# Two blocks of a transformer on one core: first products by token tile, and the rms norms as late factors

## Chip, cores and metric

The kernel runs on one core of a Trainium2 chip. The metric is the device time of one execution in microseconds (us); the median of the runs is given. The core's engines, each with a queue of its own that it works off in order, are TensorE (PE; its weight loads are PEld), VectorE (DVE), ScalarE (ACT), GpSimd (POOL) and SyncE (SP), which here issues the weight loads.

## What is computed

256 tokens of width 2048 and a context of 256 more pass through a first block of two layers, and the 256 tokens then through a second block. All is float32.

```python
# first block, layer l (layer 0 on x and ctx, layer 1 on x alone beside k and v of ctx)
h    = x * (1 + scale_l) + shift_l                 # scale, shift, gate from silu(c) @ w_mod[l]
parts = h @ w_in[l]                                # conv, q, k, v, gates, pool
out  = concat(conv, attention, pool) @ w_out[l]
x    = layernorm(ALPHA * x + gate_l * out) * ln_g[l] + ln_b[l]
# second block
hn = rms_norm(x, norm_mix_g)                       # x * rsqrt(mean(x*x) + 1e-6) * g
q_a, k_a, v_a, q_b, k_b, v_b, f, g_a, g_b = split(hn @ w_in_2)
merged = sigmoid(g_a) * (moba(q_a, k_a, v_a) @ w_proj_a) + sigmoid(g_b) * (fox(q_b, k_b, v_b, f) @ w_proj_b)
x  = x + merged @ w_out_2
hm = rms_norm(x, norm_mlp_g)
x  = x + square(relu(hm @ w_up)) @ w_down
return rms_norm(x, norm_final_g)
```

## The kernel before

Every weight passes once through the core. `fetch` (L171 to L187) loads a chunk of 128x1024 floats (two K tiles of 512 columns, or four of 256) and splits it: ScalarE casts it to a rounded half `hi` (L185), VectorE subtracts to get the residue `lo` (L186). Raw chunks, hi and lo have three buffers each. A product is three matmuls, hi·hi, hi·lo and lo·hi (`mm3`, L246 to L249). Activations lie transposed (channels on partitions) in `Act` tiles, again as hi and lo (`split`, L337).

Two routines do the products. `lin_b` (L251) holds blocks of 128 weight columns, and its result has channels on partitions and tokens along the row; with 256 tokens hi and lo of the activation go in one matmul, and VectorE sums the two halves afterwards (L306, L315). `lin_a` (L279) holds tiles of 128 tokens, and its result has tokens on partitions. Both go chunk by chunk, all blocks or tiles for one chunk, in five accumulators. With `hold=3` the last three chunks of a `lin_a` are done tile by tile, so that the first tile is ready before the last one.

The end of a layer is `mix_out` (L797): five column blocks, the last with hold 3; each tile's rows z get gate, residual and statistics (L818 to L820), and after the last block `ln_coef` (L826) makes mean and 1/std, with a power on GpSimd (L123). What follows must turn the rows into a transposed activation:

- Layer 0 to layer 1: `next_layer` (L902 to L925) scales the rows of all four tiles (L906 ScalarE, L908 VectorE), transposes (L913), applies gain and shift of the layer norm and of the modulation (L915, L916), splits (L339, L340); two steps run before layer 1's first products, six behind their chunks. GpSimd makes x1 = the x rows with gain and shift (L923, L924) and stores it.
- Layer 1 to the second block: `norm_rows` (L932) applies the layer norm to the rows with gain and shift (L945, L946; the last quarter of tile 1 by ScalarE and GpSimd), sums squares (L850) and makes the factor 1/rms. `norm_T` (L985) multiplies the rows by it (L992, L994), transposes (L1000) and splits (L1002, L1003). The first three residues of the group behind are GpSimd's.
- Before w_up: the same `norm_T`, once all of x is summed and squared (L1168, L850).

The order of the instructions on an engine is mainly the program's; a scheduler in the build moves some of them past others. Work between chunks is queued: `later` and `bg_step` run one step of a generator behind each chunk, `deferred` runs a function some chunk ends later.

## Time and profile before

| | |
|---|---|
| median of 3 runs | 2932.58 us (2932.4 to 2933.4) |
| profiled execution, its own time | 2930.09 us |
| span, first to last instruction | 2928.3 us |
| TensorE busy | 2871.4 us, 98% of the span |
| VectorE busy | 1946.9 us, 66% |
| ScalarE busy | 1179.6 us, 40% |
| GpSimd busy | 249.3 us, 9% |
| mean granted TensorE clock | 0.993 |

The span is 2.5 us below the median of the runs, so the two are not mixed. An engine that is busy 66% of the span may still be the one that is waited for in a short stretch: there one reads the waits and the order, not the share.

### The profile page before, as it was taken

The numbers are of one execution on the slowest core, as the hardware profiler recorded it, in microseconds if no ns is written. First come the engines' busy times: TensorE is split into PE (matmuls) and PEld (weight loads), VectorE is DVE, ScalarE is ACT, GpSimd is POOL, SyncE is SP. The second block draws the span as 40 slices with busy tenths as digits, with TensorE's granted clock in tenths as the row PEclk, the third lists the DMA queues.
The fourth block names the chain that finished last, engine by engine and source line by source line (L and its number), as shares of the span: only waits on it lengthen the run. The fifth ranks groups of instructions, "written<-read, shape, count | busy, mean of one in ns | idle before, by whom it ended". The sixth has DMA issues, their size and how long they took to land.

```text
span 2928.3 us, 38793 instructions
## 1 busy us (share of the span) xinstructions
PE 2871.4 (98%) x14898; PEld 2371.6 (81%) x14898; DVE 1946.9 (66%) x2890; ACT 1179.6 (40%) x1688; POOL 249.3 (9%) x287
## 2 busy tenths in 40 slices
PE   8999999999999999999969999999999999999998
PEld 5677777777879788888868888888888888888887
DVE  3779987887885658477675555766656556455564
ACT  3123432432322435244434454544445434344443
POOL 0000001001100410012110000001101101010011
PEclk9999999999999999999989999999999999999999
DMA  8764445455754445456744545455555555656554
GB/s 307 268 205 143 134 159 173 158 162 180 243 196 133 133 137 194 155 164 200 238 140 166 187 157 184 156 188 180 196 191 173 194 187 186 200 185 192 191 189 166
DMA packets 156433, 533.84 MB, mean 182 GB/s; under 512 B 17860, under 2 KB 21196, under 8 KB 156248
## 3 DMA queue, kind: packets, MB, share of 16 engines
q1 hardware_dynamic: 148656, 510.79, 52.8%
q0 software_dynamic: 5632, 18.36, 2.1%
q8 instruction: 116, 1.90, 0.3%
q10 hardware_dynamic: 1960, 2.22, 0.3%
q14 instruction: 69, 0.57, 0.1%
HBM read 527.07 MB, written 4.23 MB: 181 GB/s over the span
## 4 chain that ended last, share of the span: by engine, by line
PE 72%; issue 5%; DVE 3%; DMA 1%; ACT 1%; POOL 1%; POOLq 0%; ACTq 0%; DVEq 0%
PE acc L267 23%; PE acc L247 11%; PE acc L269 11%; PE acc L249 11%; PE acc L248 11%; PE aux L658 1%; PE aux L690 1%; DVE lo L186 1%; DVE ma L406 1%; PE aux L680 0%; POOL small L123 0%; PE aux L1077 0%; ACT hi L185 0%; DMA raw<-in_w_in_dram 0%; DVE small L660 0%
## 5 line engine op out<-in xcount | busy, mean ns | idle before, releaser
L186 DVE TENSOR_TENSOR lo<-raw,hi 128x1024 fp32r<-128x1024 f32 x766 | 937.2, 1227 | 679.2 <-ACT hi L185 676.9
L185 ACT CAST hi<-raw 128x1024 fp32r<-128x1024 f32 x769 | 805.5, 1050 | 1352.5 <-PE acc L249 457.9
L267 PE MATMUL acc<-act,hi 128*128 128x512 f32 x2960 | 1050.0, 399 | 0.7 <-DVE qs L306 0.7
L269 PE MATMUL acc<-act,lo 128*128 128x256 f32 x2960 | 829.3, 281 | 0.0
L267 PEld LDWEIGHTS acc<-act,hi 128*128 128x128 f32 x2960 | 555.2, 188 | 139.7 <-issue 5.1
L247 PE MATMUL acc<-hi,act 128*128 128x512 f32 (+1 forms) x1568 | 582.7, 372 | 1.5 <-ACT act L339 1.3
L249 PE MATMUL acc<-hi,act 128*128 128x512 f32 (+1 forms) x1568 | 578.3, 369 | 0.5 <-DVE act L340 0.5
L248 PE MATMUL acc<-lo,act 128*128 128x512 f32 (+1 forms) x1568 | 578.1, 369 | 0.2 <-DVE lo L186 0.2
L269 PEld LDWEIGHTS acc<-act,lo 128*128 128x128 f32 x2960 | 558.0, 189 | 1.8 <-DVE lo L186 0.2
L406 DVE SCALAR_TENSOR_TENSOR ma<-mod,cc,ma 128x512 f32<-128x512 f32 x480 | 339.1, 744 | 28.1 <-DMA mod<-in_w_mod_dram 26.7
L247 PE MATMUL acc<-act,hi 128*128 128x512 f32 x896 | 357.3, 399 | 0.0
L249 PE MATMUL acc<-act,lo 128*128 128x512 f32 x896 | 350.3, 391 | 0.0
L248 PE MATMUL acc<-act,hi 128*128 128x512 f32 x896 | 350.0, 391 | 0.0
L247 PEld LDWEIGHTS acc<-hi,act 128*128 128x128 f32 x1568 | 296.5, 189 | 54.9 <-issue 4.0
L249 PEld LDWEIGHTS acc<-hi,act 128*128 128x128 f32 x1568 | 296.2, 189 | 50.2 <-DVE act L340 1.1
L248 PEld LDWEIGHTS acc<-lo,act 128*128 128x128 f32 x1568 | 296.7, 189 | 49.4 <-DVE lo L186 1.2
L247 PEld LDWEIGHTS acc<-act,hi 128*128 128x128 f32 x896 | 168.2, 188 | 52.7 <-ACT hi L185 8.8
L249 PEld LDWEIGHTS acc<-act,lo 128*128 128x128 f32 x896 | 168.2, 188 | 39.1 <-issue 3.7
L248 PEld LDWEIGHTS acc<-act,hi 128*128 128x128 f32 x896 | 168.5, 188 | 35.7 <-issue 3.0
L315 DVE TENSOR_REDUCE tmp<-acc 128x256 f32<-128x512 f32 x169 | 112.8, 683 | 52.4 <-PE acc L269 52.4
L1184 POOL TENSOR_TENSOR tmp<-tmp 128x256 f32<-128x256 f32 x64 | 69.8, 1090 | 565.7 <-ACT tmp L1183 538.5
L340 DVE TENSOR_TENSOR act<-tmp,act 128x256 fp32r<-128x256 f32 (+1 forms) x96 | 58.4, 615 | 45.8 <-ACT act L339 45.7
(209 smaller groups left out, 1648.8 us busy)
## 6 DMA issues: line engine op xcount, KB each, us to landing
raw<-in_w_in_dram SPq DMA_DIRECT2D x384, 512.0 KB, 3.5
mod<-in_w_mod_dram SPq DMA_DIRECT2D x158, 512.0 KB, 4.2
raw<-in_w_up_dram SPq DMA_DIRECT2D x128, 512.0 KB, 4.3
raw<-in_w_down_dram SPq DMA_DIRECT2D x128, 512.0 KB, 4.3
raw<-in_w_out_dram SPq DMA_DIRECT2D x96, 512.0 KB, 4.3
mod<-in_w_mod_dram SPq DMA_DIRECT2D x68, 256.0 KB, 5.2
raw<-in_w_proj_a_dram SPq DMA_DIRECT2D x16, 512.0 KB, 3.5
raw<-in_w_proj_b_dram SPq DMA_DIRECT2D x16, 512.0 KB, 4.0
```

The lines of the kernel that those rows point to most:

```text
L185: S.copy(hi, raw)
L186: (fn or V).tensor_sub(lo, raw, hi)
L247: mm(ps, lh, rh, start=start, stop=False)
L248: mm(ps, lh, rl, start=False, stop=False)
L249: mm(ps, ll, rh, start=False, stop=stop)
L267: mm(p[:w, :].rearrange("p (a t) -> p a t", a=2), hi[:, kk, c:c + w], act.both(k0 + kk, tok), start=start, stop=False)
L269: mm(p[:w, :ntok], lo[:, kk, c:c + w], ah[:, tok], start=False, stop=stop)
L315: V.reduce_sum(t, ps[0], axis=AX.X)
L340: V.tensor_sub(lo, src, h)
L406: V.scalar_tensor_tensor(st[s], raw[:, kk, :], cc2[:, k, s:s + 1], st[s], op0=ALU.mult, op1=ALU.add)
L658: mm(p[:, :nk], a[r, q0:q0 + P], b[r, 0:nk], start=n == 0, stop=n == 2)
L1184: G.tensor_mul(t, t, t)
```

## The change

`lin_a` gets a `lead`: its first three chunks, too, can be done tile by tile, with a `hook` called behind each chunk of a tile. Where a new activation is needed, the rows of the early tiles are scaled and turned by such hooks, between products of the late tiles: behind layer 0, the context's tiles 0 and 1 between tile 3's last products; behind layer 1, tile 0 between tile 1's. `turn_T` turns two K tiles at a time. An `Act` takes its tiles one by one.

In the second block the norm's 1/rms no longer scales the rows. Gain and shift of layer 1's norm and the gain of the rms norm are applied to the transposed values (for the shift and gain, columns `lng1` and `lnb1` are added to the small parameters). x2 itself and its squares are made later (`norm_mix`). `row_factors` makes 1/rms as a row over the tokens, in all partitions, by a product of a matrix of ones with a diagonal; a product group's result is multiplied by it (tokens along the row) or scaled by the column (tokens on partitions). In w_up the relu becomes max and multiplication on VectorE. GpSimd makes no residues any more.

```diff
@@ lin_a, its callers' arguments left out
-    def lin_a(act, tiles, consume, korder=K16, mid=None, hold=1):
+    def lin_a(act, tiles, consume, korder=K16, mid=None, hold=1, lead=0, hook=None):
-        for ks in [[k] for k in korder[:cut]] + [korder[cut:]]:
+        for ks in [korder[:lead]][:lead] + [[k] for k in korder[lead:cut]] + [korder[cut:]]:
...
+                    if hook and len(ks) > 1:
+                        hook(i, ks.index(k0))
@@ first transition
+    def scale_rows(i, nt, z=z0):
+        t, (m, r, nb) = z[i, nt], z[i]
+        if i % 2:
+            S.activation(t, t, AF.Identity, scale=r, bias=nb)
+        else:
+            V.tensor_scalar(t, t, r, nb, op0=ALU.mult, op1=ALU.add)
+    def turn_T(act, z, tiles, kt, c1, c0, tok):
+        n = len(tiles)
+        ps, f = aux(), tmp(2 * n * P)
+        for k in range(2):
+            for j, i in enumerate(tiles):
+                o = (n * k + j) * P
+                nc.tensor.transpose(ps[:, o:o + P], z[i, kt // 4][:, (kt % 4 + k) * P:(kt % 4 + k + 1) * P], ident)
+        for k in range(2):
+            o = slice(k * n * P, (k + 1) * n * P)
+            g, b = c1[:, kt + k:kt + k + 1], c0[:, kt + k:kt + k + 1]
+            if k:
+                S.activation(f[:, o], ps[:, o], AF.Identity, scale=g, bias=b)
+            else:
+                V.tensor_scalar(f[:, o], ps[:, o], g, b, op0=ALU.mult, op1=ALU.add)
+        split(act.two(kt, tok), f.rearrange("p (k t) -> p k t", k=2))
...
+    def done0(i, z, cf):
+        z0.update(z)
+        z0[i] = cf
...
+        if i < 2:
+            for nt in range(2):
+                scale_rows(i, nt)
+        else:
+            scale_rows(i, 0)
...
+    def hook0(i, k):
+        if i == 3:
+            turn(2 * k, 0)
...
+    def lead0(i, k):
+        n = 3 * i + k
+        if n == 1:
+            for j in (2, 3):
+                scale_rows(j, 1)
+        elif n in (3, 4, 5):
+            turn(2 * (n - 3), 1)
+        elif n in (6, 7):
+            turn(6, n - 6)
+            for j in (2 * n - 12, 2 * n - 11):
+                scale_rows(j, 2)
+        elif n in (8, 9):
+            turn(8, n - 8)
...
+        turn(10, 0)
+        turn(10, 1)
+        for j in range(4):
+            scale_rows(j, 3)
+        yield
+        for kt in (12, 14):
+            turn(kt, 0)
+            turn(kt, 1)
+            yield
...
-            for i, (m, r, nb) in coef.items():
-                if i % 2:
-                    S.activation(z[i, nt], z[i, nt], AF.Identity, scale=r, bias=nb)
-                else:
-                    V.tensor_scalar(z[i, nt], z[i, nt], r, nb, op0=ALU.mult, op1=ALU.add)
-            for b in range(4):
-                kt = 4 * nt + b
-                ps = aux()
-                for i in range(4):
-                    nc.tensor.transpose(ps[:, i * P:(i + 1) * P], z[i, nt][:, b * P:(b + 1) * P], ident)
-                f = tmp()
-                S.activation(f[:, CTX], ps[:, CTX], AF.Identity, scale=fs[:, kt, 0:1], bias=fb[:, kt, 0:1])
-                V.tensor_scalar(f[:, X], ps[:, X], fs[:, kt, 1:2], fb[:, kt, 1:2], op0=ALU.mult, op1=ALU.add)
-                split(hT[kt], f)
-                if b % 2:
-                    yield
@@ second transition, its removed lines first
-    def norm_rows(i, z, coef):
-        ss = sums5()
-        m, r, nb = coef
-        for nt in POOLED[i]:
-            t = z[i, nt]
-            S.activation(t, t, AF.Identity, scale=r, bias=nb)
-            G.tensor_mul(t, t, lng1[nt])
-            G.tensor_add(t, t, lnb1[nt])
-        for nt in range(4):
-            t = z[i, nt]
-            if nt not in POOLED[i]:
-                V.scalar_tensor_tensor(t, t, m, lng1[nt], op0=ALU.subtract, op1=ALU.mult)
-                V.scalar_tensor_tensor(t, t, r, lnb1[nt], op0=ALU.mult, op1=ALU.add)
-                square_sum(t, ss, nt)
-        for nt in POOLED[i]:
-            square_sum(z[i, nt], ss, nt)
-        rs[i] = rms(ss)
...
+    def turn1(kt, *tiles):
+        turn_T(hn, z1, tiles, kt, gb1[:, :KT], gb1[:, KT:], slice(tiles[0] * P, (tiles[-1] + 1) * P))
+    def done1(i, z, cf):
+        z1.update(z)
+        z1[i] = cf
+        for nt in range(2):
+            scale_rows(i, nt, z1)
+    def hook1(i, k):
+        if i == 1 and k < 2:
+            turn1(2 * k, 0)
...
+    x2 = mix_out(1, Y, lambda i, nt: x1[i * P:(i + 1) * P, nt * 512:(nt + 1) * 512], done1, hook1)
+    turn1(4, 0)
...
+    def row_factors(n, ss, wait):
+        dg = []
+        for i in range(2):
+            rs[n, i] = rms(ss[i])
+            dg.append(tmp(P))
+            V.tensor_scalar(dg[i], ident, rs[n, i], None, op0=ALU.mult)
+        one = tmp(P)
+        G.memset(one, 1.0)
+        def spread():
+            p = aux()
+            for i in range(2):
+                mm(p[:, i * P:(i + 1) * P], one, dg[i], start=True, stop=True)
+            S.copy(rsr[n], p[:, :T])
+        deferred.append([wait, spread])
+    def lead1(i, k):
+        n = 3 * i + k
+        if n < 3:
+            turn1(2 * n, 1)
+        elif n == 3:
+            turn1(6, 0, 1)
+            for j in range(2):
+                scale_rows(j, 2, z1)
+        elif n == 5:
+            turn1(8, 0, 1)
+    def norm_mix():
+        ss = [sums5(), sums5()]
+        for j in range(2):
+            scale_rows(j, 3, z1)
+        for kt in (10, 12, 14):
+            turn1(kt, 0, 1)
+            yield
+        for nt in range(4):
+            for i in range(2):
+                t = x2[i, nt]
+                V.tensor_mul(t, t, lng1[nt])
+                V.tensor_add(t, t, lnb1[nt])
+                square_sum(t, ss[i], nt)
+            yield
+        row_factors(0, ss, 4)
+        for t, i in early:
+            S.activation(t, t, AF.Copy, scale=rs[0, i])
@@ the factors
     def norm_T(act, xs, rs, gain):
...
-                t = t32()
-                if i:
-                    S.activation(t, xs[i, nt], AF.Copy, scale=rs[i])
-                else:
-                    V.tensor_scalar(t, xs[i, nt], rs[i], None, op0=ALU.mult)
-                n.append(t)
...
-                S.activation(t, val(ps), AF.Copy, scale=HD_SCALE)
+                V.scalar_tensor_tensor(t, val(ps), HD_SCALE, rsr[0], op0=ALU.mult, op1=ALU.mult)
...
-            S.activation(t, val(ps), AF.Sigmoid)
+            V.tensor_mul(t, val(ps), rsr[0])
+            S.activation(t, t, AF.Sigmoid)
...
+        if (c0 + n) % 512 == 0:
+            later(norm_T(hm, x2, c0 // 512, "nlg"))
+    row_factors(1, ss, 6)
...
-                S.activation(t, val(ps), AF.Relu)
+                V.scalar_tensor_tensor(t, val(ps), 0.0, rsr[1], op0=ALU.max, op1=ALU.mult)
```

How the instructions stand, at the three places where waits are worked out below. First VectorE at the end of layer 0, from the coefficients of tile 2 on (L818 is L829 of the changed kernel, L186 is L185, L340 is L351). Before:

```order
L908 TENSOR_SCALAR p_6628<-p_6628,small 128x512 [waits DVE_49]
L908 TENSOR_SCALAR p_6960<-p_6960,small 128x512
L186 TENSOR_TENSOR lo<-raw,hi 128x1024 [waits DMAHW4_49,Activation_49]
L186 TENSOR_TENSOR lo<-raw,hi 128x1024 [waits DMAHW5_49,Activation_49]
L818 TENSOR_TENSOR tmp<-acc,row 128x256 [waits PE_49]
L186 TENSOR_TENSOR lo<-raw,hi 128x1024 [waits DMAHW6_49,Activation_49]
L819 SCALAR_TENSOR_TENSOR p_7556<-p_7556,tmp 128x256 [waits DVE_49]
L908 TENSOR_SCALAR p_7276<-p_7276,small 128x512
L820 BN_STATS bn<-p_7556 128x6 [waits DVE_49]
L908 TENSOR_SCALAR p_7554<-p_7554,small 128x512
```

After:

```order
L955 TENSOR_SCALAR tmp<-aux,fs,fb 128x256 [waits PE_49]
L939 TENSOR_SCALAR p_6631<-p_6631,small 128x512 [waits DVE_49]
L185 TENSOR_TENSOR lo<-raw,hi 128x1024 [waits DMAHW4_49,Activation_49]
L351 TENSOR_TENSOR act<-tmp,act 128x2x256 [waits DVE_49,Activation_49]
L955 TENSOR_SCALAR tmp<-aux,fs,fb 128x256 [waits PE_49]
L185 TENSOR_TENSOR lo<-raw,hi 128x1024 [waits DMAHW5_49,Activation_49]
L955 TENSOR_SCALAR tmp<-aux,fs,fb 128x256 [waits PE_49]
L829 TENSOR_TENSOR tmp<-acc,row 128x256
L185 TENSOR_TENSOR lo<-raw,hi 128x1024 [waits DMAHW6_49,Activation_49]
L351 TENSOR_TENSOR act<-tmp,act 128x2x256 [waits DVE_49,Activation_49] x2
L830 SCALAR_TENSOR_TENSOR p_7559<-p_7559,tmp 128x256 [waits DVE_49]
```

The scaled transposed pairs (L955) and their residues (L351) now stand among the residues of the next weights (L185), and tile 3's last column block (L829, L830) behind them.

Second, TensorE around the end of layer 1 (`acc_12959` and `acc_12962` are tile 1's last column block, `ident` marks a transpose, `hi_13177` the first weights behind). Before:

```order
L249 MATMUL acc_12959<-hi_12992,act_12307 128x256
L1000 MATMUL aux_13147<-ident_105,p32_13143 128x128 [waits DVE_49]
L1000 MATMUL aux_13152<-ident_105,p32_13143 128x128
L1000 MATMUL aux_13157<-ident_105,p32_13143 128x128
L1000 MATMUL aux_13147<-ident_105,p32_13145 128x128 [waits Activation_49]
L1000 MATMUL aux_13152<-ident_105,p32_13145 128x128
L1000 MATMUL aux_13157<-ident_105,p32_13145 128x128
L247 MATMUL acc_13173<-hi_13177,act_13141 128x512 [waits Activation_49]
```

After, still within tile 1's second of three held chunks:

```order
L246 MATMUL acc_12962<-hi_12965,act_12326 128x256
L948 MATMUL aux_13061<-ident_105,p32_12347 128x128 [waits DVE_49]
L948 MATMUL aux_13061<-ident_105,p32_12347 128x128
L247 MATMUL acc_12962<-lo_12966,act_12326 128x256
L248 MATMUL acc_12962<-hi_12965,act_12326 128x256
L948 MATMUL aux_13082<-ident_105,p32_12347 128x128 x2
L246 MATMUL acc_12962<-hi_12995,act_12326 128x256
```

Transposes of tile 0's rows (`p32_12347`) have moved in among tile 1's products; before, all of them stood behind the last one.

Third, VectorE at a change of product groups in w_up. Before:

```order
L315 TENSOR_REDUCE tmp<-acc 128x256 [waits PE_49]
L186 TENSOR_TENSOR lo<-raw,hi 128x1024 [waits DMAHW1_49,Activation_49]
L315 TENSOR_REDUCE tmp<-acc 128x256 [waits PE_49]
L340 TENSOR_TENSOR act<-tmp,act 128x256 [waits Activation_49]
L315 TENSOR_REDUCE tmp<-acc 128x256 [waits DVE_49,PE_49]
L186 TENSOR_TENSOR lo<-raw,hi 128x1024 [waits DMAHW2_49,PE_49,Activation_49]
```

After (L317 is L315, L1292 is new):

```order
L317 TENSOR_REDUCE tmp<-acc 128x256 [waits PE_49]
L185 TENSOR_TENSOR lo<-raw,hi 128x1024 [waits DMAHW1_49,Activation_49]
L1292 SCALAR_TENSOR_TENSOR tmp<-tmp,cs 128x256 [waits DVE_49]
L317 TENSOR_REDUCE tmp<-acc 128x256 [waits PE_49,Pool_49]
L1292 SCALAR_TENSOR_TENSOR tmp<-tmp,cs 128x256 [waits DVE_49]
L317 TENSOR_REDUCE tmp<-acc 128x256 [waits PE_49]
L351 TENSOR_TENSOR act<-tmp,act 128x256 [waits Activation_49] x2
L1292 SCALAR_TENSOR_TENSOR tmp<-tmp,cs 128x256 [waits DVE_49]
L317 TENSOR_REDUCE tmp<-acc 128x256 [waits DVE_49,PE_49]
L185 TENSOR_TENSOR lo<-raw,hi 128x1024 [waits DMAHW2_49]
```

Behind each sum (L317) comes the multiplication by the factors (L1292); the third sum now stands behind two of them, and the residue of the chunk after next (the second L185) behind three and the fourth sum.

## Rows read from the trace of the kernel before

**Rows 1.** Waits of TensorE: line, waited for: us in total, times, longest.

```profile
PE aux L1000 <- ACT p L992: 13.0, 2, 9.3
PE aux L1000 <- DVE small L830: 12.6, 1, 12.6
PE aux L913 <- ACT p L906: 5.9, 1, 5.9
...
PE aux L1000 <- DVE act L1003: 0.7, 1, 0.7
```

**Rows 2.** By stage: us, busy of PE, PEld, DVE, ACT, POOL, clock, DMA share, GB/s.

```profile
953.59:1014.56 60.97, 53.76 (x259) 44.32 (x258) 43.97 (x50) 29.44 (x47) 33.29 (x30) 0.94 0.46 142
1512.42:1562.93 50.51, 28.55 (x130) 23.01 (x130) 34.87 (x51) 23.74 (x46) 11.21 (x9) 0.76 0.28 94
2197.82:2231.40 33.58, 29.14 (x162) 25.20 (x160) 19.73 (x33) 17.97 (x31) 3.62 (x8) 0.90 0.53 173
```

**Rows 3.** Timeline of ScalarE behind layer 0: start, length, line, operation, idle before.

```profile
1002.04 1.05 ACT L185 CAST hi<-raw 128x1024 fp32r<-128x1024 f32 x1 [2.08 <-PE acc L249]
...
1008.37 1.05 ACT L185 CAST hi<-raw 128x1024 fp32r<-128x1024 f32 x1 [1.51 <-PE acc L249]
```

**Rows 4.** Timeline of ScalarE, first group of the second block.

```profile
1544.23 1.05 ACT L185 CAST hi<-raw 128x1024 fp32r<-128x1024 f32 x1 [1.41 <-PE acc L249]
...
1547.45 1.05 ACT L185 CAST hi<-raw 128x1024 fp32r<-128x1024 f32 x1 [1.43 <-PE acc L249]
```

**Rows 5.** Timeline of VectorE, first two groups of w_up.

```profile
2219.78 1.22 DVE L186 TENSOR_TENSOR lo<-raw,hi 128x1024 fp32r<-128x1024 f32 x1 [1.25 <-ACT hi L185]
...
2223.04 1.22 DVE L186 TENSOR_TENSOR lo<-raw,hi 128x1024 fp32r<-128x1024 f32 x1 [1.26 <-ACT hi L185]
...
2229.31 0.69 DVE L315 TENSOR_REDUCE tmp<-acc 128x256 f32<-128x512 f32 x1 [1.00 <-PE acc L269]
...
2251.92 0.69 DVE L315 TENSOR_REDUCE tmp<-acc 128x256 f32<-128x512 f32 x1 [1.34 <-PE acc L269]
```

**Rows 6.** Timeline of VectorE behind layer 0.

```profile
952.18 1.01 DVE L908 TENSOR_SCALAR p<-p,small 128x512 f32<-128x512 f32 x2
...
968.41 1.81 DVE L340 TENSOR_TENSOR act<-tmp,act 128x512 fp32r<-128x512 f32 x1 [0.69 <-ACT act L339]
...
972.54 0.99 DVE L916 TENSOR_SCALAR tmp<-aux,fs,fb 128x256 f32<-128x256 f32 x2
...
973.77 1.29 DVE L340 TENSOR_TENSOR act<-tmp,act 128x512 fp32r<-128x512 f32 x2 [0.23 <-ACT act L339]
```

**Rows 7.** Timeline of ScalarE behind layer 0, scaling, shifting and casts.

```profile
959.76 1.52 ACT L906 ACTIVATE p<-p,small 128x512 f32<-128x512 f32 x2 [4.88 <-DVE small L832]
...
971.27 1.01 ACT L915 ACTIVATE tmp<-aux,fb,fs 128x256 f32<-128x256 f32 x2
...
973.11 1.14 ACT L339 CAST act<-tmp 128x512 fp32r<-128x512 f32 x2 [0.83 <-DVE tmp L916]
```

**Rows 8.** Timeline of VectorE at the end of layer 1.

```profile
1508.15 0.42 DVE L818 TENSOR_TENSOR tmp<-acc,row 128x256 f32<-128x256 f32 x1 [2.02 <-PE acc L249]
...
1508.61 0.42 DVE L819 SCALAR_TENSOR_TENSOR p<-p,tmp 128x256 f32<-128x256 f32 x1
...
1511.13 2.37 DVE L832 SCALAR_TENSOR_TENSOR small<-small 128x1 f32<-128x1 f32 x1 [0.47 <-POOL small L123]
```

**Rows 9.** Timeline of GpSimd at the same place.

```profile
1511.12 4.66 POOL L186 TENSOR_TENSOR lo<-raw,hi 128x1024 fp32r<-128x1024 f32 x2
```

**Rows 10.** Timeline of VectorE, second change of groups in w_up.

```profile
2252.53 1.21 DVE L186 TENSOR_TENSOR lo<-raw,hi 128x1024 fp32r<-128x1024 f32 x1
...
2255.12 0.69 DVE L315 TENSOR_REDUCE tmp<-acc 128x256 f32<-128x512 f32 x1
...
2255.73 1.22 DVE L186 TENSOR_TENSOR lo<-raw,hi 128x1024 fp32r<-128x1024 f32 x1
```

**Rows 11.** Group of the page: GpSimd's squarings; busy, mean ns, idle before.

```profile
L1184 POOL TENSOR_TENSOR tmp<-tmp 128x256 f32<-128x256 f32 x64 | 69.8, 1090 | 565.7 <-ACT tmp L1183 538.5
```

More of the change, by code (lines that the diff above doesn't have):

```diff
@@ L321, in __init__, with slot, two @@
         def __init__(self, n, w):
-            self.w, self.per = w, 2048 // w
-            self.t = [p_act.tile([P, 2, 2048], F32R, tag="act", name="act") for _ in range(n // self.per)]
+            self.w, self.per, self.t = w, 2048 // w, {}
+        def slot(self, kt):
+            s = kt // self.per
+            if s not in self.t:
+                self.t[s] = p_act.tile([P, 2, 2048], F32R, tag="act", name="act")
+            return self.t[s], (kt % self.per) * self.w
         def __getitem__(self, kt):
-            j = (kt % self.per) * self.w
-            t = self.t[kt // self.per]
+            t, j = self.slot(kt)
             return t[:, 0, j:j + self.w], t[:, 1, j:j + self.w]
+        def two(self, kt, tok):
+            t, j = self.slot(kt)
+            return tuple(t[:, i, j:j + 2 * self.w].rearrange("p (k t) -> p k t", k=2)[:, :, tok] for i in range(2))
         def both(self, kt, tok):
-            j = (kt % self.per) * self.w
-            return self.t[kt // self.per][:, :, j + tok.start:j + tok.stop]
+            t, j = self.slot(kt)
+            return t[:, :, j + tok.start:j + tok.stop]
     new_act = Act
@@ L502, in tile_two_blocks, with layer @@
     ALL, CTX, X = slice(0, 512), slice(0, 256), slice(256, 512)
-    def layer(l, hT):
+    def layer(l, hT, **first):
         both = l == 0
@@ L795, in layer, with mix_out @@
         return [Y[i] for i in range(16)]
-    def mix_out(l, Y, resid, done):
+    def mix_out(l, Y, resid, done, hook=None):
         both = l == 0
@@ L857, in rms, with plan_second @@
         return rsqrt(v)
+    O2 = dict(qa=0, ka=1024, va=2048, qb=3072, kb=4096, vb=5120, f=6144, ga=6152, gb=8200)
+    W2 = ("w_in_2",)
+    ORDER2 = [("va", 0), ("va", 1), ("qa", 0), ("ka", 0), ("qa", 1), ("ka", 1), ("vb", 0), ("vb", 1), ("f", 0),
+              ("qb", 0), ("kb", 0), ("qb", 1), ("kb", 1)]
+    K8 = list(range(0, 8, CHUNK))
+    def plan_second():
+        for n, g in ORDER2:
+            if n == "f":
+                stream.extend(entries(W2, O2[n], 8, [0], nk=KT))
+            else:
+                plan(W2, O2[n] + 512 * g, 512, K16)
+        for j in range(4):
+            plan(W2, O2["ga"] + 512 * j, 512, K16)
+        for j in range(4):
+            plan(("w_proj_a_2",), 512 * j, 512, K8)
+        for j in range(4):
+            plan(W2, O2["gb"] + 512 * j, 512, K16)
+            plan(("w_proj_b_2",), 512 * j, 512, K8)
+        stream.extend(block_entries(("w_out_2",)))
+        for q in range(4):
+            for j in range(4):
+                plan(("w_up_2",), q * 2048 + j * 512, 512, K16)
+            if q < 3:
+                for j in range(4):
+                    plan(("w_down_2", q), j * 512, 512, K16)
+            else:
+                stream.extend(block_entries(("w_down_2", q)))
     stream.extend(mod_first(1, *GROUPS[0], TAGS) + mod_first(0, *GROUPS[0], TAGS))
@@ L1007, in tile_two_blocks @@
-    hn = new_act(KT, 256)
-    later(norm_T(hn, x2, rs, "nmg"))
-    bg(2)
+    hn = new_act(KT, 256)
+    z1 = {}
+    gb1 = p_sm.tile([P, 2 * KT], F32, tag="gb1", name="gb1", bufs=1)
+    for n, o in (("lng1", 0), ("lnb1", KT)):
+        V.tensor_mul(gb1[:, o:o + KT], smc(n, 0, KT), smc("nmg", 0, KT))
+    def turn1(kt, *tiles):
[5 more added lines that the diff above has]
+            scale_rows(i, nt, z1)
@@ new lines, in hook1, with norm_T @@
+    def hook1(i, k):
[3 more added lines that the diff above has]
+    turn1(4, 0)
+    rs, rsr = {}, [cs[:, :T], cs[:, T:2 * T]]
+    def norm_T(act, xs, nt, gain):
+        for b in range(4):
+            kt = nt * 4 + b
+            ps = aux()
+            for i in range(2):
+                nc.tensor.transpose(ps[:, i * P:(i + 1) * P], xs[i, nt][:, b * P:(b + 1) * P], ident)
+            h, lo = act[kt]
+            S.activation(h, ps[:, :T], AF.Copy, scale=smc(gain, kt))
+            V.scalar_tensor_tensor(lo, ps[:, :T], smc(gain, kt), h, op0=ALU.mult, op1=ALU.subtract)
+            if b % 2:
+                yield
@@ L1010, in tile_two_blocks @@
+    later(norm_mix())
     TK = slice(0, 256)
@@ L1032, in c @@
             vv[n, i, g] = qs_tile()[:, :512] if n == "va" else t32()
-            S.copy(vv[n, i, g], ps)
-        lin_a(hn, [0, 1], c)
+            if (0, i) in rs:
+                S.activation(vv[n, i, g], ps, AF.Copy, scale=rs[0, i])
+            else:
+                S.copy(vv[n, i, g], ps)
+                early.append((vv[n, i, g], i))
+        lin_a(hn, [0, 1], c, **(dict(lead=LEAD, hook=lead1) if (n, g) == ORDER2[0] else {}))
     fc = cst.tile([P, T], F32, name="fc")
```

102 lines of the change are left out of this document (33 added, 69 removed).

## The prediction

> **What bounds the kernel now.** I began with busy time by engine (the table above): TensorE is busy 98% of the span, so only what lets it wait or slows its clock can be won. The list of who waited for whom comes next: TensorE's dearest waits are all for the transposes of a new activation, at the change of layer (L913) and at the two places where the second block normalises (L1000) [rows 1]. I call them A (layer 0 to layer 1, about 954 us), B (layer 1 to the second block, 1512 us) and C (before w_up, 2198 us). A table by stage, from the last product before each to the end of the first product group behind it, shows the granted clock there at 0.94, 0.76 and 0.90 on average [rows 2]; of its two levels, 2.4 and 1.2 GHz, the lower one was granted for part of each window, and besides there only after the very last products.
>
> What each place costs is the window less eight chunks at the steady pace of the same group. A: casts of weight chunks follow at 6.33 us, 8 of them are 50.6; the window is 61.0, the loss 10.3 [rows 2, 3]. B: pace 3.22, 25.8 of 50.5, the loss 24.7 [rows 2, 4]. C: pace 3.26; the first block's sum starts at 2229.3, and at pace it would at 2197.8 + 26.1 - 2.1 (three blocks of a chunk of 22.61 / 8 us lie behind it) = 2221.8; the loss is 7.5 [rows 5]. Together 42.5 us. No other entry of that list is larger, and the change touches none of the others.
>
> **A, part by part.** The transposes stay 64, at (3.26 - 22.61 / 8) / 4 = 0.11 us each; 12 now stand between the last tile's products and find their rows scaled. Gone is the wait for tile 3's scaled rows. New is the queue on VectorE, in front of the first group's weights. From 952.2, where the old kernel scaled tile 2 [rows 6], I add up its new order: a scaled pair 0.49, rows 0.48, the residue of chunk 0 1.14 (1.22 less the 0.08 by which neighbours overlap), the pair's residue 0.64, and so on [rows 6, 10]. That gives the third pair's residue at 959.9, and tile 3's statistics only at 963.5. ScalarE's order puts the second pair's cast behind two weight casts (0.50 + 0.57 + 1.05 + 0.50 + 1.05 + 0.57 [rows 3, 7], with one wait for VectorE), at 957.6. TensorE, done with tile 3 at 955.1, starts tile 0 at once. It waits 0.6 for the second pair, 1.4 for tile 3's rows (963.5 + 0.76 for the scaling [rows 7]; it is there at 963.0), 0.2 for the first x pair, then 0.8, 0.4 and 0.5 for residues: GpSimd by then makes x1, and a residue costs 1.81 instead of 0.64 [rows 6]. The fourth chunk must wait for the first one's buffers, since three are held: 0.8. Sum 4.7, and 0.8 for hand-overs: 5.5. Bounds: 2.5 (only tile 3's rows and the residues) and 10.3 (nothing won).
>
> **B.** Gone are two passes of 128x512 for gain, shift, squares and 1/rms before the first transpose, and three residues on GpSimd, beside which a 128x1 operation took 2.37 us instead of some 0.16 [rows 8, 9]. In their place: tile 0 ends at 1508.1 [rows 8], statistics and GpSimd's power take 2.8 (at most the 3.0 between the rows), one scaling 0.48; its first transpose can run at 1511.5, TensorE stands there at 1510.7 (it holds back two products): 0.8. The rest of tile 1 ends about 1513.9; the pair's cast stands on ScalarE behind the casts of chunks 1 and 2, the last of which needs a buffer that tile 1 frees at 1513.6: 1513.7 + 1.05 + 0.4 = 1515.2, wait 1.3. Chunk 2 and the third pair: 0.8. Tile 1's rows need its coefficients (VectorE at 1519.6, behind two residues), then three scalings on ScalarE of 0.7: waits of 0.3, 0.5, 0.7 and 0.3. Chunk 3: 0.2. Then gain and shift of x2, now 16 passes of 0.64 beside residues of 1.22 a chunk: they run 0.5 late once. Sum 5.4. The row factors add two products of 128x128, unseen before: 0.11 each as a transpose, 0.40 as a product four times as wide, taken 0.25, so 0.5. With 1.0 for hand-overs 6.9. Bounds 4 and 15 (half the old loss, if the orders above slip).
>
> **C.** The transposes of three quarters move into w_out_2's groups, the last quarter behind the first chunks, and no 1/rms stands before them. TensorE has the first two chunks ready (three buffers, as now): 0.4, and 0.5 for its row factors: 0.9, between 0.6 and 3.
>
> **Elsewhere.** 1/rms becomes a 128x256 multiplication on VectorE at 0.42 [rows 8]: 4 for each of 32 product groups of 22.6 us (8 q and k, 8 gates, 16 w_up), 1.7 us a group. VectorE has the room (busy 20 of 33.6 us in C's window [rows 2]); what counts is the change of groups. There five accumulators allow the next group's fourth block only when the third sum is read. In the old kernel that sum starts 3.20 us after the first and ends at 3.9; TensorE asks at 2.1 + 2.1 = 4.2 [rows 5, 10]. In w_up two multiplications and no third residue now stand before it: it ends between 3.9 and 4.4. The residue of the chunk after next moves from 5.0 to about 7.4, and is due at 7.9. So 0 to 0.5 a group; near the lower end, 0.15 for 16 groups and 0.07 for the others: 3.5. Bounds: -1 (ScalarE loses 80 passes, the relus and q's scalings) and 19 (0.5 at all w_up groups, and 0.7 at the rest).
>
> Costs taken as nothing: x1's stores come later on GpSimd, whose first reader is layer 1's output, 400 us away; two tiny multiplications move to the start, where VectorE waits anyway; SP's order of weight loads stays, and a raw buffer is free a residue after its cast, well before its chunk.
>
> The old multiplication groups show one more thing: a residue that began before GpSimd's squaring kept its 1.22 [rows 10], and the squarings, 1.09 on average [rows 11], are the longer for it. The Trainium skill (SBUF — State Buffer, Who interferes with whom) says that a VectorE instruction with two SBUF inputs and a GpSimd instruction that reads SBUF exclude each other, whoever starts first blocking the other for its whole length; the 2.37 above agrees. It speaks against this change, whose new multiplication has two SBUF inputs and runs right beside those squarings. What that would do here, from rows, is the second rival.
>
> **Sum.** 5.5 + 6.9 + 0.9 + 3.5 = 16.8 stay of 42.5; 25.7 are won. The profiled execution took 2930.1 (span 2928.3): 2904.4. The median of the runs is 2.5 above it: 2907.
>
> **Rivals.**
> 1. The lead groups stay bound. If VectorE and ScalarE drag both groups (A 8, B 12) and the clock falls in the broken stretch (1520 to 1524 in B holds little but transposes), about 3 us each in both, as C's loss less its waits of 4.4 (13.0 - 9.3, and 0.7 [rows 1]) suggests, 13.6 less is won: about 2920. For it: B's long chain; against: no single wait above 1.4.
> 2. The squarings block the multiplications. In w_up the second multiplication of a group then waits for the first squaring, up to 0.6 more in front of the third sum: 16 x 0.6 = 9.6, 2917. For it: the sum has 0.3 us of room; against: TensorE's total wait for sums is nearly nil today, and VectorE came first there.
> 3. Slower: late factors cost more than the waits. If each of the 32 groups held TensorE for all its 1.7 us, 54 would be paid for the 29 won at A, B and C: +25, 2958. It decides from 29 / 32 = 0.9 us a group. Against: only a part of one boundary's work stands in front of an accumulator.
> 4. All waits vanish but the row factors' products and the first hand-overs: 40 won, 2893. For it: the new orders leave TensorE work at nearly every wait.
>
> **Chances.** Forecast 0.60 (own range 2898 to 2915), rival 1 0.16, rival 2 0.08, rival 4 0.10, rival 3 0.06. A measurement can tell 0.2% (5.9 us) from no change: faster than 2926.7 are the forecast, rival 4, and most of rivals 1 and 2 (0.13 and 0.06), 0.89 together; within 0.2% 0.05; slower 0.06. The range 2896 to 2922 leaves out most of rival 4 (0.09), and above it rival 3 and a third of rival 1 (0.11).
>
> **What would show it.** Right: no wait of TensorE above 2 us at A, B or C; the clock at 1.0 in C's window and near it in A and B; the first group behind B ending some 37 us after tile 0's last product there, and not 55; w_up groups at 22.6 to 22.9 us. Wrong: clock at 1.2 GHz in A or B; groups behind w_up's changes above 23.1 us with waits for a sum of VectorE; the fourth chunk of a lead group late by more than 2 us.

## The result, and the profile after

The changed kernel takes 2904.57 us (median of 4 runs, 2901.11 to 2906.42) against 2932.99 of the old one beside it: 0.9902 of its time, 95% interval 0.9889 to 0.9914. Forecast were 2907, range 2896 to 2922. The profiled execution took 2906.42 us (span 2904.6), forecast 2904.4. The sum was nearly met, but two of its four terms were far off and cancelled: A won about half of what was forecast, and the loss expected elsewhere did not come.

The waits of TensorE that answer to [rows 1] (line, waited for: us in total, times, longest). These lines are totals of the whole kernel and hold all that is left at A and B; one wait of 1.3 in the first line and one of 0.2 in the fourth lie elsewhere:

```profile
PE acc L246 <- ACT act L350: 3.1, 3, 1.3
...
PE aux L948 <- ACT tmp L953: 1.8, 2, 1.2
...
PE acc L246 <- ACT hi L184: 0.9, 1, 0.9
...
PE acc L247 <- DVE lo L185: 0.8, 2, 0.6
PE aux L948 <- DVE p L939: 0.7, 1, 0.7
PE aux L948 <- ACT p L937: 0.6, 2, 0.4
```

At A 3.5 us are left (0.5, 0.4, 1.2, 0.9, 0.6 in order of time) and at B 2.9 (0.7, 1.3, 0.3, 0.6), where the old kernel's longest waits were 12.6, 9.3 and 5.9. The three stages, as in [rows 2] (us, busy of PE, PEld, DVE, ACT, POOL, clock, DMA share, GB/s), from the last product before each to the end of the first group behind it:

```profile
958.15:1015.50 57.35, 53.79 (x242) 42.40 (x242) 41.68 (x47) 27.68 (x45) 32.84 (x30) 0.94 0.44 150
1515.30:1543.60 28.30, 26.10 (x123) 20.64 (x124) 27.41 (x48) 22.94 (x42) 0.76 (x3) 1.00 0.50 166
2183.50:2207.40 23.90, 23.90 (x144) 21.02 (x143) 14.32 (x21) 10.82 (x16) 0.77 (x4) 1.00 0.58 198
```

B took 28.3 us instead of 50.5, and C 23.9 instead of 33.6, both at full clock. A hardly moved, 57.4 from 61.0, and its clock is 0.94 still. Where the 1.2 GHz lie shows in finer windows of the changed kernel:

```profile
977.00:980.00 3.00, 2.89 (x15) 2.18 (x13) 3.00 (x3) 0.00 (x0) 3.00 (x5) 1.00 0.05 19
980.00:983.00 3.00, 1.01 (x5) 0.70 (x5) 1.72 (x4) 2.27 (x4) 1.96 (x4) 0.90 0.89 235
983.00:986.00 3.00, 2.43 (x6) 1.60 (x6) 2.57 (x2) 2.82 (x4) 1.66 (x2) 0.50 0.95 341
986.00:989.00 3.00, 3.00 (x9) 2.32 (x8) 3.00 (x4) 0.13 (x1) 3.00 (x2) 0.50 0.67 240
989.00:992.00 3.00, 3.00 (x15) 2.42 (x14) 3.00 (x3) 1.92 (x5) 3.00 (x3) 0.96 0.22 75
```

It was granted from 982.4 to 989.2 us, in the first profile; in the profile of its repeat (run `again` below) the stretch is half as long:

```profile
980.00:983.00 3.00, 1.20 (x4) 0.69 (x3) 2.47 (x4) 2.73 (x5) 0.54 (x2) 0.91 0.79 214
983.00:986.00 3.00, 3.00 (x9) 2.37 (x8) 3.00 (x3) 1.24 (x2) 3.00 (x2) 0.52 0.99 337
986.00:989.00 3.00, 3.00 (x15) 2.45 (x14) 3.00 (x4) 2.05 (x4) 3.00 (x2) 1.00 0.40 149
```

What ended ahead of it is in the timeline of VectorE (the last line is the first of the two residues alone), and of GpSimd and ScalarE beside it:

```profile
968.85 2.65 DVE L351 TENSOR_TENSOR act<-tmp,act 128x512 fp32r<-128x512 f32 x2
...
973.54 6.40 DVE L351 TENSOR_TENSOR act<-tmp,act 128x512 fp32r<-128x512 f32 x2 [0.35 <-ACT act L350]
...
973.54 5.80 DVE L351 TENSOR_TENSOR act<-tmp,act 128x512 fp32r<-128x512 f32 x1 [0.35 <-ACT act L350]
```

```profile
973.75 2.55 POOL L1015 TENSOR_TENSOR p<-p,row 128x512 f32<-128x512 f32 x2
976.25 2.53 POOL L1016 TENSOR_TENSOR p<-p,row 128x512 f32<-128x512 f32 x2
```

```profile
980.43 0.56 ACT L953 ACTIVATE tmp<-aux,fb,fs 128x256 f32<-128x256 f32 x1 [6.40 <-DVE tmp L955]
981.03 0.62 ACT L350 CAST act<-tmp 128x512 fp32r<-128x512 f32 x1
981.55 1.04 ACT L184 CAST hi<-raw 128x1024 fp32r<-128x1024 f32 x1
```

Two residues of split pairs (L351) took 6.40 us together, beside GpSimd's gain and shift for x1 (L1015, L1016). One of them took 5.80 of it: it began 0.2 us before four passes of GpSimd, by the trace, and ended only after the fourth; the other took 0.7. ScalarE stood behind them: its next pair (L953) waited for VectorE, and the fourth chunk's cast behind that came at 981.55, although its buffer was free from about 976, when tile 3's products of the first chunk ended. TensorE waited 1.2 us for that pair, 0.9 for the cast and 0.6 for the chunk's residue; the clock fell in the second of these waits.

At w_up, VectorE at the change of groups that answers to [rows 10], and the squarings that answer to [rows 11]:

```profile
2250.05 0.69 DVE L317 TENSOR_REDUCE tmp<-acc 128x256 f32<-128x512 f32 x1 [1.34 <-PE acc L268]
...
2252.12 0.69 DVE L317 TENSOR_REDUCE tmp<-acc 128x256 f32<-128x512 f32 x1
2252.84 0.42 DVE L1292 SCALAR_TENSOR_TENSOR tmp<-tmp,cs 128x256 f32<-128x256 f32 x1
2253.18 0.68 DVE L317 TENSOR_REDUCE tmp<-acc 128x256 f32<-128x512 f32 x1
```

```profile
L1293 POOL TENSOR_TENSOR tmp<-tmp 128x256 f32<-128x256 f32 x64 | 52.9, 826 | 574.2 <-DVE tmp L1292 567.5
```

The third sum ends 3.81 us after the first one's start (2253.18 + 0.68 - 2250.05); in the old kernel it was 3.89. It did not get later. The squarings are shorter, 0.83 on average: three of four now lie beside sums (0.61 each) and only the fourth beside residues (1.47).

Where the time went, stage by stage: ScalarE casts the 769 weight chunks in the same order in both kernels, so the k-th cast tells how far each is (casts are counted from 0). Difference of the changed kernel to the old one, us, in the first profile and in that of its repeat:

| up to | first profile | repeat | repeat, change from the row above |
|---|---|---|---|
| before A (cast 80) | +2.4 | +0.8 | |
| behind A (154) | +0.9 | -1.4 | -2.2 |
| before B (272) | +1.3 | -1.5 | 0 |
| behind B (304) | -18.8 | -21.6 | -20.1 |
| before w_out_2's transposes (488) | -17.1 | -19.9 | +1.7 |
| first w_up group done (528) | -24.4 | -27.1 | -7.2 |
| last (768) | -23.7 | -26.2 | +0.8 |

The old kernel's profiled execution took 2930.09 us (its span is 2928.3), 2.5 less than the median of its first runs, so these differences come out smaller than those of the medians; at which place the 2.5 us lie is not known.

### The profile page after: what moved, and what is told of

Same layout as the page of the kernel before. It is cut to its first block, busy times and chain, and to the rows that moved or that the text cites. A ratio compares the mean times of both kernels' runs of the same rounds, so it can differ in the third digit from the quotient of the medians.

```text
span 2904.6 us, 38908 instructions
## 1 busy us (share of the span) xinstructions
PE 2874.7 (99%) x14906; PEld 2371.7 (82%) x14906; DVE 1990.2 (69%) x3032; ACT 1157.8 (40%) x1613; POOL 221.0 (8%) x284
## 4 chain that ended last, share of the span: by engine, by line
PE 75%; DVE 3%; issue 2%; ACT 1%; DMA 1%; POOL 0%; POOLq 0%; ACTq 0%; DVEq 0%
PE acc L266 23%; PE acc L246 12%; PE acc L247 12%; PE acc L248 12%; PE acc L268 12%; DVE lo L185 1%; PE aux L669 1%; PE aux L701 1%; DVE ma L417 1%; PE aux L691 0%; PE aux L1185 0%; ACT hi L184 0%; POOL small L122 0%; DMA raw<-in_w_in_dram 0%; DVE small L671 0%
## 5 line engine op out<-in xcount | busy, mean ns | idle before, releaser
L185 DVE TENSOR_TENSOR lo<-raw,hi 128x1024 fp32r<-128x1024 f32 x769 | 948.5, 1236 | 659.6 <-ACT hi L184 658.6
L317 DVE TENSOR_REDUCE tmp<-acc 128x256 f32<-128x512 f32 x185 | 124.5, 686 | 56.4 <-PE acc L268 56.4
L1293 POOL TENSOR_TENSOR tmp<-tmp 128x256 f32<-128x256 f32 x64 | 52.9, 826 | 574.2 <-DVE tmp L1292 567.5
L677 ACT ACTIVATE pp<-aux,small 128x512 f32<-128x512 f32 (+1 forms) x96 | 58.2, 612 | 52.8 <-DVE small L673 52.7
```

The source lines that it names most:

```text
L185: (fn or V).tensor_sub(lo, raw, hi)
L317: V.reduce_sum(t, ps[0], axis=AX.X)
L677: S.activation(t, ps[i][:, :nk], AF.Exp, bias=nm[:, i:i + 1], scale=QK_SCALE, accum_out=sums[:, i:i + 1])
L1293: G.tensor_mul(t, t, t)
```

## Experiments

Every kernel is the changed kernel with one edit, but for the old kernel with x1 held back and the last one, which has two edits. Medians are of 4 or 5 runs if nothing else is said, beside the old kernel on the same chip; the old kernel's medians there lie between 2932.7 and 2933.5. "By the casts" means as in the table above, against the profile of the repeat.

**The changed kernel again.**

> The changed kernel with no edit, as the yardstick for the three that run beside it. First series: median 2904.6, single runs 2901.1 to 2906.4, a wider spread than the old kernel's 2932.4 to 2935.0. Theory of chance dips: in the first profile the clock fell to 0.81 to 0.84 at 525 to 535 us, in layer 0, behind a wait of 1.3 us that the old kernel has too (1.2 us, clock 1.0); if that dip is chance, it is absent in some profiles, and such runs are some 1.6 us shorter. Rival: it belongs to the change (other buffers, other order) and comes each time. Median expected 2902 to 2907 by both.

2904.30 (2901.33 to 2906.27). The dip at 525 us did not come: the yardstick's profile is 1.6 us ahead behind it (cast 80). Of the twelve profiles of the changed kernel and its variants, which share layer 0, two have the dip (the first and undo_A). So it is chance, and a first part of the spread. A second part lies at A: behind the same collision the clock stayed low for 6.8 us in five profiles and for 3.4 in four.

**x1 held back.** One column of the last split pair, times zero, is added to each x1 tile first:

```diff
+        h14 = hT1.both(14, slice(0, 1))
+        V.tensor_scalar(hold, h14[:, 0].bitcast(F32), 0.0, None, op0=ALU.mult)
...
+                G.tensor_add(t[:, :1], t[:, :1], hold)
                 G.tensor_mul(t, t, g)
```

> GpSimd's gain and shift for x1 behind layer 0 may start only when the last pair of layer 1's activation is split (a column times zero is added to each of its eight tiles). Theory 1: in the changed kernel's first group of layer 1, two residues of 128x512 on VectorE took 6.40 us together beside GpSimd's multiplications (1.3 where GpSimd rests); ScalarE's weight cast stood behind them, the fourth chunk came late, TensorE waited 1.2 + 0.9 + 0.6 us, and the clock fell to 1.2 GHz for some 6.3 us (half of that lost, 3.1). All of it goes: 5 to 6 us faster than the run without edit beside it, clock 1.0 throughout the place, no residue above 0.8 us there. Rival 2: the fourth chunk is late by VectorE's own queue or by the three weight buffers; then at most 1 us is won, the waits stay above 2 us in sum, and the clock falls as before.

2896.85 (2894.09 to 2897.34), ratio to the old kernel 0.9875 (0.9862 to 0.9889): 7.4 us faster than the repeat beside it, and the runs of the two don't overlap. By the casts (80 to 154), 6.2 of it at A. The same two places on VectorE, and the windows:

```profile
966.78 1.28 DVE L351 TENSOR_TENSOR act<-tmp,act 128x512 fp32r<-128x512 f32 x2
...
970.23 1.29 DVE L351 TENSOR_TENSOR act<-tmp,act 128x512 fp32r<-128x512 f32 x2 [0.66 <-ACT act L350]
```

```profile
977.00:980.00 3.00, 3.00 (x17) 2.52 (x16) 3.00 (x5) 2.12 (x4) 0.00 (x0) 1.00 0.82 236
980.00:983.00 3.00, 3.00 (x16) 2.48 (x15) 1.67 (x3) 0.99 (x3) 0.00 (x0) 1.00 0.77 270
983.00:986.00 3.00, 3.00 (x18) 2.61 (x17) 2.67 (x4) 2.95 (x5) 0.00 (x0) 1.00 0.05 20
```

A pair of residues takes 1.28 and 1.29 us instead of 2.65 and 6.40, the clock stays at 1.0, and of TensorE's waits at A two of 0.5 and 0.4 us are left. Theory 1 holds, and this is the fastest version. What it won beyond 6.2 us is not the edit's: some 0.7 lie at the gates (last section), the rest within the spread. In all nine profiles that keep the new order at A and leave x1 alone, one residue there takes 5.8 us (5.78 to 5.80); with the old order (undo_A, the old kernel) none takes more than 2.3.

**The same on the old kernel** (x1 moved behind the last pair there too, and held).

> The old kernel with x1 held back in the same way (until the last pair of layer 1's activation is split). Theory: there the place is bound by the one wait of 5.9 us for tile 3's scaled rows, and its residues of 1.8 us instead of 0.64 lie beside products: no difference from the old kernel's 2933.3, within 2 us; so it is the change that brought GpSimd's passes into a bound stretch. Rival: the collision cost the old kernel as much as the changed one, and it gets 5 to 7 us faster.

2930.97 (10 runs), ratio 0.9995 (0.9985 to 1.0005): no difference. TensorE's wait of 5.9 us at A is there as before. But the old kernel's collision at A is a lighter one: VectorE and GpSimd took turns, residue by residue and pass by pass, and no residue took more than 2.11 us. In the unedited old kernel:

```profile
981.02 3.50 DVE L340 TENSOR_TENSOR act<-tmp,act 128x512 fp32r<-128x512 f32 x2 [0.23 <-ACT act L339]
...
980.99 2.99 POOL L924 TENSOR_TENSOR p<-p,row 128x512 f32<-128x512 f32 x2
```

This lighter collision cost nothing. The residue of 5.8 us came only with the change's order; what it would have cost beside the old wait of 5.9 us no run shows.

**A undone.**

```diff
-    Y = layer(1, hT1, lead=LEAD, hook=lead0)
+    bg(2)
+    Y = layer(1, hT1)        # done0, next_layer as in the old kernel
```

> The changed kernel with the old transition between layer 0 and layer 1 (all rows scaled behind the last tile, two steps before the first products, six behind their chunks); the rest as changed. By the prediction A is worth 4.8 us (10.3 less 5.5): 4.8 slower than the run without edit beside it. By the two traces, whose weight casts behind A stand 1.4 to 1.7 us nearer, it is worth only that: 1.4 to 1.7 slower.

2906.99 (2905.23 to 2908.22), 2.7 slower than the repeat; by the casts 2.1. Neither number was met; the result lies nearer to that of the traces. Its clock was low for 6.8 us at A, the repeat's for 3.4.

**C undone.** norm_T, its place and the relu as in the old kernel.

> The changed kernel with the old way before w_up: rows multiplied by 1/rms, then turned, two steps before the first product; relu on ScalarE without a factor. q, k, v and gates keep their late factors. By the prediction C is worth 6.6 us and the factors at w_up's 16 groups cost 2.4: 4.2 slower than the run without edit. By the two traces C gave 7.1 and w_up lost 0.6 or less: 6.5 slower. Rival (late factors dear): were the factors at w_up above 0.4 us a group, undoing would win, and the kernel would be no slower.

2910.97 (2909.53 to 2913.38), 6.7 slower; by the casts 7.3 at C, with nothing lost or won behind it. So C alone gave that, and the factors of w_up cost nothing to set against it.

**w_up's factors, none and twice.**

```diff
-                V.scalar_tensor_tensor(t, val(ps), 0.0, rsr[1], op0=ALU.max, op1=ALU.mult)
+                S.activation(t, val(ps), AF.Relu)                                  # none
+                v = val(ps)                                                        # twice
+                V.tensor_mul(v, v, rsr[1])
+                V.scalar_tensor_tensor(t, v, 0.0, rsr[1], op0=ALU.max, op1=ALU.mult)
```

> w_up without its row factor (leaves out the multiplication by 1/rms there): relu on ScalarE, as in the old kernel. By the prediction the factors cost 0.15 us at each of 16 groups: 2.4 faster than 2904.3. By the two traces w_up lost at most 0.6 in all: no difference, within 0.6. Its squarings on GpSimd should be long again (median 1.20 us as in the old kernel, 0.61 now), since they fall beside residues.

> w_up with one more multiplication of 128x256 by the row factor on VectorE (the product is scaled by it twice): a quarter more work of that kind in front of the third sum, 2 x 0.4 us. By the prediction's sum the third sum now ends 3.9 to 4.4 us behind the first one's start and TensorE asks at 4.2: with 0.8 more it is late by 0.5 to 1.0 at 16 groups, 8 to 16 slower than 2904.3, with waits of TensorE for a sum. Rival: the accumulators are not what binds there, and VectorE catches up behind the boundary: under 2 slower.

None: 2904.17 (2902.20 to 2907.58), with the squarings at 1.20 us in the median again; twice: 2905.06 (2903.89 to 2908.03), both no different from 2904.3. In the second, VectorE's third sum ends 6.19 us behind the first one's start, two us after TensorE should ask for its accumulator, and TensorE waits for no sum there:

```profile
2226.05 0.69 DVE L317 TENSOR_REDUCE tmp<-acc 128x256 f32<-128x512 f32 x1 [1.35 <-PE acc L268]
...
2231.56 0.68 DVE L317 TENSOR_REDUCE tmp<-acc 128x256 f32<-128x512 f32 x1
```

The order of the built program says why. TensorE's fourth block of the new group (`acc_19593`) has been put behind the third chunk's first product, with both of the first two chunks at once; in the unedited kernel it stands right behind the third block:

```
10829 L266 MATMUL acc_19592<-act_18724,hi_19515 128x512 [waits DVE_49]
10833 L266 MATMUL acc_19590<-act_18724,hi_19537 128x512 [waits Activation_49]
...
10845 L266 MATMUL acc_19590<-act_18724,hi_19596 128x512 [waits Activation_49]
10846 L266 MATMUL acc_19593<-act_18724,hi_19515 128x512 [waits DVE_49,PE_49]
```

The scheduler in the build has moved TensorE's products past the late accumulator.

**B: the tile order.** First `lead` taken out of the first group:

```diff
-        lin_a(hn, [0, 1], c, **(dict(lead=LEAD, hook=lead1) if (n, g) == ORDER2[0] else {}))
+        lin_a(hn, [0, 1], c)     # lead1's steps: two before the group, three behind its chunks
```

> The changed kernel, but the first group of the second block goes chunk by chunk again (both token tiles for each chunk): tile 1's first two pairs are turned before the first product, the next three steps behind the first three chunks; late factors and tile 0's early pairs stay. Theory 1: at B it is the tile order that covers tile 1's statistics: its coefficients come at 1520.5 us, some 4 us behind the first product, its first pair 3 us later, and chunk by chunk only 1.4 us of tile 0's products stand in between; TensorE waits 5 to 6 us in one piece and the clock falls behind it (3 more): 7 to 9 slower than the unedited kernel's 2904.3. Theory 2: it is the late factors (no gain, shift, squares before the transposes) that won B's 20 us, and the order matters little: under 3 slower.

2904.82, and at B the casts gain and lose nothing to the repeat (under 0.1). On the two theories this settled nothing, though it shows that `lead` itself is not needed at B: the scheduler had put tile 0's three chunks ahead of tile 1's transposes here as well, so TensorE's order was unedited. The next kernel ties the tiles together in the data, by one transposed accumulator for both:

```diff
-        if i == 1 and k < 2:
-            turn1(2 * k, 0)
...
+        turn1(0, 0, 1)
+        turn1(2, 0, 1)
```

> The changed kernel, but at B both token tiles of a pair of K tiles are turned together, as in the old kernel (nothing of tile 0 among tile 1's products; one accumulator of transposes and one cast hold both tiles, so no product starts before tile 1's rows are scaled); the late factors stay. In the order of its instructions all transposes of the first pairs stand behind tile 1's last product, which the run lead0_B did not reach: there the order on TensorE stayed the unedited one. Theory 1 (the tile order covers the statistics): tile 1's coefficients come at about 1520.5 us; scaling, turning, shift and cast put the first product at some 1523 instead of 1516.6, TensorE waits 7 to 8 us and the clock falls behind it: 8 to 11 slower than 2904.3, about half of B's gain of 20. Theory 2 (the late factors alone won B): under 4 slower.

2910.16 (2909.79 to 2910.98), 5.9 slower, by the casts 4.9 at B: between the two theories. TensorE's wait at tile 1's rows, and the clock:

```profile
PE aux L948 <- ACT p L937: 6.9, 2, 6.6
```

```profile
1514.00:1518.00 4.00, 1.31 (x12) 1.07 (x10) 4.00 (x5) 1.68 (x2) 0.00 (x0) 1.00 0.36 113
1518.00:1522.00 4.00, 0.13 (x1) 0.13 (x2) 2.27 (x8) 1.00 (x2) 0.64 (x3) 0.70 0.86 283
1522.00:1526.00 4.00, 3.61 (x15) 3.12 (x16) 3.19 (x7) 3.97 (x8) 0.00 (x0) 0.50 0.00 0
1526.00:1530.00 4.00, 4.00 (x19) 3.24 (x18) 3.59 (x7) 3.01 (x5) 0.00 (x0) 0.94 0.00 0
```

There is a wait of 6.6 us in one piece, and 1.2 GHz, both much as theory 1 had it. But the clock fell while TensorE still waited, where it costs nothing, and of the changed kernel's four waits there (2.9 us) only 0.4 are left beside the long one, so the price is less than its 8 to 11.

**B: the late factors.** Rows get gain, shift, squares and 1/rms before they are turned, tile by tile (`n1` holds the scaled rows):

```diff
+        for nt in range(4):
+            t = z[i, nt]
+            V.scalar_tensor_tensor(t, t, m, lng1[nt], op0=ALU.subtract, op1=ALU.mult)
+            V.scalar_tensor_tensor(t, t, r, lnb1[nt], op0=ALU.mult, op1=ALU.add)
+            square_sum(t, ss, nt)
+        rs[0, i] = rms(ss)
```

> The changed kernel with B's late factors undone and its tile order kept: each tile's rows get layer norm with gain and shift, squares and 1/rms before they are turned (VectorE two passes for each of four quarters, ScalarE the squares), q, k, v, f and gates go without factors; w_up keeps its factor. In the order of its instructions tile 0's three chunks still stand ahead of tile 1's transposes. pairs_B put the tile order at 5.9 of B's gain of about 20. If the two parts add up, the late factors are worth the other 14: 2918. Worked out from rows: 8 passes of some 0.6 behind tile 0's statistics, then squares and power, 7 us more before tile 0's first transpose, and the same again for tile 1, against 5 us of tile 0's products in between: 12 to 16 slower than 2904.3, clock at 1.2 GHz for some us. Rival: tile 0's passes hide beside tile 1's last products, and the late factors matter little: under 6 slower (then neither part alone would matter, each covering for the other).

2918.06 (2915.86 to 2920.14), 13.8 slower, by the casts 14.6 at B. The waits, and the clock from 1513.5 us on:

```profile
PE aux L948 <- DVE p L1053: 8.0, 1, 8.0
PE acc L246 <- ACT act L350: 6.1, 4, 3.6
```

```profile
1513.50:1537.50 24.00, 13.41 (x36) 9.79 (x37) 18.62 (x40) 11.83 (x29) 3.05 (x4) 0.57 0.19 66
```

TensorE waited 8.0 us before tile 0's first transpose and 3.6 before tile 1's products, and the clock was at 1.2 GHz for most of the stretch, in the waits and behind them. With pairs_B it nearly adds up to the 20.1 that the casts show for B: 4.9 + 14.6 = 19.5. Both runs keep the first residues on VectorE, and the next one shows that this has a price of its own.

**B: residues back on GpSimd.**

```diff
+                if (n, g) == ORDER2[0]:
+                    for i in range(-len(K16), -len(K16) + 3):
+                        stream[i] = (*stream[i][:5], G)
```

> The changed kernel, but the residues of the first three weight chunks of the second block's first group are GpSimd's again, as in the old kernel. Theory 1 (VectorE and GpSimd hold each other up where both read SBUF): they start at about 1511 us, 2.3 us each, beside tile 0's statistics and scaling, whose 128x1 operation took 2.37 us there in the old kernel against 0.16 now; tile 0's first transpose and all behind it come 2 to 4 us later: 2 to 5 slower than 2904.3. Theory 2: VectorE is the bound of this place, and three residues of 1.22 fewer on it bring tile 1's coefficients forward: 1 to 3 faster. Between them: no difference.

2910.74 (2909.31 to 2912.56), 6.4 slower; by the casts 4.8 at B, as theory 1 had it, and the rest lies before B, where the edit changes nothing. Timelines of VectorE and of GpSimd in that run:

```profile
1511.91 3.37 DVE L942 TENSOR_SCALAR p<-p,small 128x512 f32<-128x512 f32 x3
...
1518.37 3.64 DVE L351 TENSOR_TENSOR act<-tmp,act 128x256 fp32r<-128x256 f32 x2
```

```profile
1511.74 2.35 POOL L185 TENSOR_TENSOR lo<-raw,hi 128x1024 fp32r<-128x1024 f32 x1
1516.26 5.47 POOL L185 TENSOR_TENSOR lo<-raw,hi 128x1024 fp32r<-128x1024 f32 x2 [2.17 <-ACT hi L184]
```

Three scalings of 128x512 took 3.37 us (0.5 each in the changed kernel) beside the first residue: one of them took 2.45 and ended 0.3 behind it. Two small residues took 3.64 (0.43 each) beside the next two. VectorE lost 4.7 us and was relieved of 3.7. TensorE waited 2.6 us for tile 0's rows instead of 0.7, and the clock was low for 3.4 us behind it. So the three parts of B are not separate: undone one by one they cost 4.9, 14.6 and 4.8, 24.3 in sum, where all of B won 20.1.

**x1 held back, and both halves of B's single pairs on VectorE.**

> x1 held back as in the run x1_late, and in addition VectorE applies gain and shift to both halves of tile 0's and tile 1's single pairs at B (ScalarE did one half, and its cast of the first pair stood behind a weight cast, 1.26 us of waiting). If that wait goes: 1 us faster than x1_late's 2896.85, so 2895 to 2896.5; if VectorE becomes the bound there (it gets five passes of 0.36 more): 1 to 3 slower than x1_late.

2899.86 (2898.43 to 2901.41). TensorE still waits 1.2 us for the first pair's cast, so the edit does not do what it was for. Of the 3 us behind x1_late the casts put 0.7 at B, 1.3 at the gates' pace and 0.7 before A. It is dropped.

## Why the prediction came out right

**A, expected 4.8, got 1.4 to 2.7** (casts, undo_A). The step that failed is the price of a residue beside x1, "1.81 instead of 0.64". That was a row of the old kernel, where residues and GpSimd's passes take turns. Here one residue was held through four passes: 5.80 us. The waits alone would have been met (4.7 forecast, 3.5 came), but with the late pair and the late fourth chunk the clock fell, for which the sum had no term; it is rival 1 for A. Half speed for 6.8 us in the first profile and 3.4 in the repeat cost up to half of that; by the casts A won 1.4 in the first and 2.2 in the repeat. Two signs of being wrong that the prediction had named came at A: 1.2 GHz, and the fourth chunk of a lead group late by more than 2 us. x1_late shows that both go with the collision.

The Trainium skill (SBUF — State Buffer, Who interferes with whom) says that of a VectorE instruction with two SBUF inputs and a GpSimd instruction that reads SBUF the one that was issued first holds the other off for its whole length. The second small residue in pool_B agrees: it began behind a residue of GpSimd, took 2.60 us and ended 0.3 behind it. The 5.80 does not fit: by the trace this residue began before the first of the four passes, and it was held through all of them. When the two engines take turns and when not stays open. I had turned that rule on w_up, where it did not bite, and not on x1, where its row stood.

**B, expected 17.8, got 20.1.** The first steps held: first transpose ready 0.7 us late (0.8 forecast), the first pair 1.26 (1.3), tile 1's coefficients at 1520.5 (1519.6). The later ones were too high: no wait for chunks 2 and 3 and the third pair (1.0 forecast), 0.9 instead of 1.8 for tile 1's rows. The allowances for hand-overs and for the gain and shift of x2 were not needed; the clock stayed at 1.0. Of rival 1 this half is refuted. The first group ended 34 us after tile 0's last product (37 forecast).

**C, expected 6.6, got 6.7 to 7.3** (undo_C): two chunks ready, the row factors' four products done in 0.36 us (0.5 forecast), no wait.

**Elsewhere, expected 3.5 lost, got nothing.** The failed step is "it ends between 3.9 and 4.4": the third sum ended at 3.81. And the question was the wrong one: up_twice makes it 6.19, and the build's scheduler steps round it. Rival 3's point, 0.9 us a group, was never near: twice the work cost 0.8 in all, less than the spread. Rival 2 fell too: the multiplications keep their 0.42, since each squaring of 0.61 is over within the sum of 0.69 that follows its multiplication. The 1.7 us lost before cast 488 are not the factors' either: by cast 448 the repeat had lost 2.2 behind B; x1_late, undo_C and up_none have the same factors at the gates and lost 0.2 (last section).

So A was some 2.5 short, B 2.3 and elsewhere 3.5 over, less one or two for the gates' pace: 28.4 between the medians for 25.7. That the median came within 2.5 us of the forecast is in part luck: the collision at A hid what was won at B and elsewhere. Rival 4's 2893 is what x1_late nearly reaches.

## What to carry to other kernels

An engine with nothing in its queue starts as soon as its data allow, not where its lines stand in the program: GpSimd's side work for x1 began at 966.7 us, right behind the transposes that read the same rows, and so lay in the one stretch where VectorE was waited for; a tie to later data that moved it out won 6 to 7 us. A collision that costs nothing in the old profile has to be priced again when the order around it changes, and at its worst case (one residue held through several passes), not at a row of the old order. Before an experiment on order runs, read the built order: a scheduler may undo the edit, or already do what the edit was to show.
